# Differential attention: half-height tiles for the rotated parts, projections a head ahead, splits and values later

## The chip, the core and the metric

The kernel runs on one NeuronCore of a Trainium2 chip. The metric is the device time of one execution in microseconds. TensorE is called PE in the profile's rows (PEld is its weight load), VectorE DVE, ScalarE ACT, GpSimd POOL, and SP is the engine that issues the DMAs.

## The reference, cut to what matters

A trunk of two layers over 512 tokens of width 1024, in fp32. Each layer has a mixer, a cross-attention into 256 memory tokens, and a feed-forward part, each followed by a layer norm. The change touches the mixer of the second layer, differential attention with rotary positions, 8 heads of two 64-wide halves each, and the memory keys and values that are computed beside it.

```python
def odd_mixer(x, w_in, lam_p, subln_g, w_out, lam_init):
    q, k, v = jnp.split(x @ w_in, 3, axis=-1)
    q, k = rope(q), rope(k)              # 8 heads x 2 halves of 64
    o = diff_attention(q, k, v, lam)     # per head: softmax(q0 k0^T/8) - lam * softmax(q1 k1^T/8), times v (128 wide)
    o = rms_norm(o, subln_g) * (1.0 - lam_init)
    return o.reshape(B_, S, C_WIDTH) @ w_out

def memory_cross_attention(x, mem, wq, wkv, wo):
    k, v = jnp.split(mem @ wkv, 2, axis=-1)
    ...
```

## The kernel before

**Arithmetic.** To get more precision than one fp32r matmul gives, an operand is split into a high part (a cast to fp32r, on ScalarE) and a low part (the rest, a subtraction, on VectorE or GpSimd). A product of two split operands is three matmuls: high x high, high x low, low x high (`mm3`, lines 143 to 145). Weights arrive in chunks of 128 x 1024 (`chunk`, lines 131 to 139): one DMA into one of two `raw` buffers, a cast into one of five `whi` tiles, a subtraction into one of five `wlo` tiles. `tproj` (157) projects all 512 tokens to 128 features, `nproj` (182) tokens first.

**The odd layer** (`odd`, 838). The projections of heads 0 and 1 come first, then the memory tokens are loaded and split (`memory`, 692; into four `part` and four `kv` tiles), then the values of all heads (line 894). Each projected bank passes `rope` (850): a copy to `raw`, four DMAs that swap quarter rows, a multiplication by the cosines on VectorE, and two operations on GpSimd (lines 858 and 859) that give the rotated tile `m`. `project_q` and `project_k` split `m` at once: for each half c, `qh` holds the high part in both 64-row halves and `ql` the low part in both, while `kst` holds the key's high part in the rows of c and its low part in the other rows. That is six 128 x 512 tiles a head out of 13 `st` buffers. Two matmuls over 128 rows then give all four products (lines 949 and 950).

**The loop** (`diff_heads`, 931; `pipe`, 122). 8 heads x 4 query blocks are 32 units, in five stages: scores (row maximum on VectorE, exponential on ScalarE, combination), the normalisation `norm` (983), the product with the values `mix` (974), the transposes of the finished head `finish` (992), and the transposes of the probabilities `turn` (962). After each stage `fill` (107) takes work from a queue of jobs until an estimate of TensorE time has been used up: the stage's figure times `rate(i)`. Unit i means pass i of this loop. The queue holds, in this order: the memory keys of all four heads (`cross_k`), the projections of heads 2 to 6, the memory values (`cross_v`), the projections of head 7, and the first half of the output projection. `before` (906) makes sure at a head's third unit that the next head's projections are out.

The order in which the code issues operations is a priority: at build time they are put into the order of each engine's queue, and a tile that has no free buffer waits until one is released. On the chip each engine works through its queue.

The same trick with half-height operands appears in one other place, the neighbourhood attention of the first layer (line 1288), whose scores contract over 64 rows:

```python
            for u in range(2):
                rows = slice(u * 64, u * 64 + 64)
                nc.tensor.matmul(sb[u][:, :256], q[rows, g * P:(g + 1) * P], k[rows, k0 * 64:k0 * 64 + 256],
                                 start=True, stop=True)
```

Of the kernel before, what the change touches and what calls it, by code (L numbers as in the profile page):

```python
# [10 lines left out]
F32 = mybir.dt.float32  # L11
F32R = mybir.dt.float32r
AF = mybir.ActivationFunctionType
ALU = mybir.AluOpType
# [32 lines left out]
class Trunk:  # L47
# [3 lines left out]
    def __init__(self, ctx, tc, a, stop=6):  # L51
        self.tc, self.nc, self.a, self.stop = tc, tc.nc, a, stop
        self.n = 0
        e = ctx.enter_context
        self.dp = e(tc.tile_pool(name="dp", bufs=1, space=bass.MemoryType.DRAM))
        self.pp = e(tc.tile_pool(name="pp", bufs=1, space=PSUM))
        self.cp = e(tc.tile_pool(name="cp", bufs=1))
        self.wp = e(tc.tile_pool(name="wp", bufs=1))
        self.sp = e(tc.tile_pool(name="sp", bufs=1))
        self.gp = e(tc.tile_pool(name="gp", bufs=1))  # L60
        self.xtp = e(tc.tile_pool(name="xtp", bufs=1))
        self.lo_eng = tc.nc.vector
        self.jobs = []
        self.late = []
        self.xr = {}

# [32 lines left out]
    def step(self):  # L99
        j = self.jobs[0]  # L100
        cost = j.step()
        if j.done:
            self.jobs.pop(0)
            return 0.0
        return cost

    def fill(self, us):
        while us > 0 and self.jobs:
# [594 lines left out]
                    p.extend([x[:, :M], x[:, M:2 * M]])  # L703
        return parts

    def even_mem(self, mem):

        pairs = [[self.wp.tile([P, 1024], F32R, tag=t, bufs=5, name=self.nm("m" + t)) for t in ("whi", "wlo")]
                 for _ in range(2)]
        tiles = [x[:, u * 512:(u + 1) * 512] for p in pairs for u in range(2) for x in p]  # L710
        mem.extend(self.memory(lambda: tiles.pop(0)))
        yield 0.0
# [14 lines left out]
                self.nc.scalar.copy(kk[:, e * M:(e + 1) * M], b[:, :M])  # L727
            ks.append(kk)

    def cross_v(self, l, vs, mem):  # L730

        for h in range(2):
            bs = yield from self.nproj([self.a["wv"][l, h, i] for i in range(4)], 512, MB, *mem)
            for b in bs:
                v = self.kvblk()
                self.nc.scalar.copy(v, b)
                vs.append(v)
# [100 lines left out]
    def odd(self, l, mk, mv):  # L838
        nc, a = self.nc, self.a
        H = 8  # L840
        halves = (slice(0, 64), slice(64, 128))
        qs, ks, parts = [None] * (2 * H), [None] * (2 * H), []
        with self.phase("odd") as pool:
            tmp = self.tiles(pool)
            cos, sin = tmp("cos", 1), tmp("sin", 1)
            nc.sync.dma_start(cos, a["rope"][0])
            nc.sync.dma_start(sin, a["rope"][1])
            nlam, gc = self.lambdas(tmp("raw", 1))

            def rope(b):  # L850
                raw, sw, m = tmp("raw", 1), tmp("sw"), tmp("m")
                nc.scalar.copy(raw, b)
                for c in range(2):
                    lo, hi = slice(c * 64, c * 64 + 32), slice(c * 64 + 32, c * 64 + 64)
                    nc.sync.dma_start(sw[lo], raw[hi])
                    nc.sync.dma_start(sw[hi], raw[lo])
                nc.vector.tensor_tensor(m, b, cos, ALU.mult)
                nc.gpsimd.tensor_tensor(sw, sw, sin, ALU.mult)
                nc.gpsimd.tensor_tensor(m, m, sw, ALU.add)
                return m  # L860

            def project_q(h, b):
                m = rope(b)
                for c in range(2):
                    s, o = halves[c], halves[1 - c]
                    qh, ql = tmp("st", 13, dt=F32R), tmp("st", 13, dt=F32R)
                    for r in (s, o):
                        nc.scalar.activation(qh[r], m[s], AF.Copy, scale=0.125)
                    for r in (s, o):
                        nc.vector.scalar_tensor_tensor(ql[r], m[s], 0.125, qh[s].bitcast(F32), ALU.mult, ALU.subtract)  # L870
                    qs[2 * h + c] = (qh, ql)

            def project_k(h, b):
                m = rope(b)
                for c in range(2):
                    s, o = halves[c], halves[1 - c]
                    kst = tmp("st", 13, dt=F32R)
                    nc.scalar.copy(kst[s], m[s])
                    nc.vector.tensor_tensor(kst[o], m[s], kst[s].bitcast(F32), ALU.subtract)
                    ks[2 * h + c] = kst  # L880

            def projects(h):
                project_q(h, (yield from self.tproj(a["ow"][h])))
                project_k(h, (yield from self.tproj(a["ow"][H + h])))

            first = self.tproj_halves([a["ow"][0], a["ow"][H], a["ow"][1], a["ow"][H + 1]])
            for i, b in enumerate(first):
                (project_k if i % 2 else project_q)(i // 2, b)
            slots = [self.part] * 4 + [lambda: self.kvblk(F32R)] * 4
            mem = self.memory(lambda: slots.pop(0)())  # L890
            vs = []
            for h in range(2):
                row = []
                for b in self.run(self.nproj([a["ov"][h, i] for i in range(4)], 512, TB, tag=("at", "pj")[h])):
                    v = tmp("v", 8)
                    nc.scalar.copy(v, b)
                    row.append(v)
                vs.append(row)
            self.lo_eng = nc.vector
            self.job(self.cross_k(l, mk, mem))  # L900
            more = [self.job(projects(h)) for h in range(2, 7)]
            self.job(self.cross_v(l, mv, mem))
            more += [self.job(projects(h)) for h in range(7, H)]
            second = self.outproj(parts, KB, a["oout"], l, 0)

            def before(h):
                if 2 <= h < H:
                    self.need(more[h - 2])

            self.diff_heads(H, before, qs, ks, vs, nlam, gc, tmp, parts)  # L910
            self.lo_eng = nc.vector
        with self.phase("ln") as pool:
            second(pool)
# [14 lines left out]
        nc.vector.tensor_scalar(gc, gc, 1.0 - LAM_INIT, None, ALU.mult)  # L928
        return nlam, gc

    def diff_heads(self, H, before, qs, ks, vs, nlam, gc, tmp, parts):
        nc = self.nc

        def scores(n):
            h, t = n["h"], n["t"]
            if t == 2:
                before(h + 1)
            if t == 0:
                n["head"] = {"ssq": self.small(4, 4)}
            else:  # L940
                n["head"] = units[h * TB]["head"]
            tk = slice(t * P, (t + 1) * P)
            nm, sm = self.small(2), self.small(2)
            rc = n["rc"] = self.small(2, 8, "rc")
            ps = n["p"] = []
            for c in range(2):
                sb = self.bank()
                qh, ql = qs[2 * h + c]
                nc.tensor.matmul(sb, qh[:, tk], ks[2 * h + c], start=True, stop=False)
                nc.tensor.matmul(sb, ql[:, tk], ks[2 * h + c], start=False, stop=True)  # L950
                nc.vector.tensor_reduce(nm[:, c:c + 1], sb, AX.X, ALU.max, negate=True)
                p = tmp(f"p{c}", 3 - c)
                nc.scalar.activation(p, sb, AF.Exp, bias=nm[:, c:c + 1], accum_out=sm[:, c:c + 1])
                ps.append(p)
            nc.vector.reciprocal(rc, sm)
            nc.vector.scalar_tensor_tensor(rc[:, 1:2], rc[:, 1:2], nlam, sm[:, 0:1], ALU.mult, ALU.mult)
            nc.vector.scalar_tensor_tensor(ps[0], ps[1], rc[:, 1:2], ps[0], ALU.mult, ALU.add)
# [8 lines left out]
        def mix(n):  # L966
            h, t, hd = n["h"], n["t"], n["head"]
            tk = slice(t * P, (t + 1) * P)
            if t == 0:
                hd["on"] = tmp("on")  # L970
                hd["ob"] = self.bank()
            ob, ssq = hd["ob"], hd["ssq"]
            for j in range(TB):
# [12 lines left out]
        def finish(n):  # L986
# [4 lines left out]
            for j in range(TB):  # L991
# [5 lines left out]

        units = [{"h": h, "t": t} for h in range(H) for t in range(TB)]
        self.pipe(units, [(scores, 0, 1.0), (norm, 4, 0.0), (mix, 3, 1.4), (finish, 5, 0.0), (turn, 2, 1.3)],
                  lambda i: 1.1 if i < 22 else 0.9)  # L1000


    def even(self, l, mk, mv):
        nc, a = self.nc, self.a
        A = 4
        with self.phase("even") as pool:
# [72 lines left out]
            def project_b(hp):  # L1079
                for i in range(2):  # L1080
                    bqk[2 * hp + i] = tiled((yield from self.tproj(a["ebqk"][4 * i + hp])), tmp("qk", 18))

            mem = []
            bjobs = [self.job(g) for g in (project_v(), project_b(0), project_b(1), self.even_mem(mem), project_b(2))]
            kv = [self.job(g) for g in (self.even_k(l, mk, mem, 0), project_b(3), self.even_k(l, mk, mem, 1),
                                        self.even_v(l, mv, mem))]
            second = self.outproj(parts, KB, a["eout"], l, 0)
# [349 lines left out]
```

## Time and profile before

| | us |
|---|---|
| median of 3 runs | 1592.86 (1592.32 to 1599.11) |
| the profiled execution | 1595.57 |
| its span, first to last instruction | 1593.9 |
| mean granted TensorE clock, of full speed | 0.996 |

The profile is of one execution. Its span lies 1.7 us under that execution's own time; the median of the other runs lies 2.7 us under it. A matmul's record lasts longer than the time it takes from its neighbours, since matmuls are pipelined: the pitch from start to start is what a matmul costs.

### The profile page before, as it was taken

To read this page: it belongs to the slowest core of one execution; us is meant where nothing else is said; L and a number is where in the kernel's file an instruction comes from. 1 tells how busy PE (TensorE), PEld (TensorE's weight loads), DVE (VectorE), ACT (ScalarE), POOL (GpSimd) and SP (SyncE) were. 2 spreads that over 40 slices of the span, in tenths; PEclk is the share of its full clock that TensorE was granted. 3 is DMA by queue.
4 is the path that set the end of the run, shared out by engine and by line. 5 is a ranking of instruction groups with operands and counts; after the bars stand their busy time and mean duration, and the time that the engine had idled before them with its cause. 6 is when DMAs were issued, how large, how long until landed. Compare 5 with 4: busy or idle time off the path is not lost.

```text
span 1593.9 us, 24998 instructions
## 1 busy us (share of the span) xinstructions
PE 1561.3 (98%) x9668; PEld 1375.4 (86%) x9668; DVE 1163.3 (73%) x1892; ACT 785.4 (49%) x1465; POOL 262.1 (16%) x263
## 2 busy tenths in 40 slices
PE   8999999999999999999999999989999999999997
PEld 7877887898899999988898977767988999999886
DVE  4684445475499989898766588776745998988986
ACT  4684455244255555445245566663442655554450
POOL 0012000221220000014131144232212100000151
PEclk9999999999999999999999999999999999999999
DMA  5432343442333333353254433403413333333531
GB/s 166 141 98 75 101 145 126 171 135 76 134 120 119 106 101 103 103 211 93 80 181 132 131 88 93 132 27 119 146 53 146 119 120 103 104 103 102 198 93 66
DMA packets 59415, 185.89 MB, mean 117 GB/s; under 512 B 7680, under 2 KB 7840, under 8 KB 59296
## 3 DMA queue, kind: packets, MB, share of 16 engines
q1 hardware_dynamic: 59296, 184.30, 35.7%
q8 instruction: 76, 1.25, 0.3%
q14 instruction: 43, 0.35, 0.1%
HBM read 167.47 MB, written 12.60 MB: 113 GB/s over the span
## 4 chain that ended last, share of the span: by engine, by line
PE 35%; DVE 6%; ACT 3%; POOL 2%; DMA 2%; issue 2%; SPq 0%; POOLq 0%; DVEq 0%; ACTq 0%
PE pj L143 3%; PE pj L145 3%; PE pj L144 3%; PE at L661 3%; PE pj L416 2%; PE pj L417 2%; PE at L531 2%; PE pj L418 2%; PE pj L531 2%; PE at L416 2%; PE at L417 2%; PE at L418 2%; PE at L143 2%; PE at L144 2%; PE at L145 2%
## 5 line engine op out<-in xcount | busy, mean ns | idle before, releaser
L137 ACT CAST whi<-raw 128x1024 fp32r<-128x1024 f32 (+2 forms) x158 | 159.3, 1009 | 194.8 <-PE pj L144 67.2
L138 DVE TENSOR_TENSOR wlo<-raw,whi 128x1024 fp32r<-128x1024 f32 (+2 forms) x142 | 170.3, 1202 | 110.6 <-ACT whi L137 104.1
L143 PE MATMUL pj<-xh,whi 128*128 128x512 f32 (+1 forms) x640 | 228.0, 356 | 0.0
L145 PE MATMUL pj<-xh,wlo 128*128 128x512 f32 (+1 forms) x640 | 216.9, 339 | 0.6 <-DVE wlo L138 0.6
L144 PE MATMUL pj<-xl,whi 128*128 128x512 f32 (+1 forms) x640 | 216.5, 338 | 0.0
L397 ACT CAST whi<-sump 128x512 fp32r<-128x512 f32 x160 | 97.6, 621 | 113.3 <-issue 64.4
L143 PEld LDWEIGHTS pj<-xh,whi 128*128 128x128 f32 x640 | 120.7, 189 | 15.7 <-issue 5.2
L144 PEld LDWEIGHTS pj<-xl,whi 128*128 128x128 f32 x640 | 120.7, 189 | 14.7 <-issue 3.8
L145 PEld LDWEIGHTS pj<-xh,wlo 128*128 128x128 f32 x640 | 120.4, 188 | 14.8 <-DVE wlo L138 0.8
L401 DVE TENSOR_TENSOR wlo<-sump,whi 128x512 fp32r<-128x512 f32 x160 | 107.7, 688 | 13.3 <-ACT whi L397 13.1
L397 ACT CAST whi<-raw 128x512 fp32r<-128x512 f32 x120 | 72.2, 617 | 32.2 <-PE at L417 14.8
L581 POOL TENSOR_TENSOR s<-kv 128x256 f32<-128x256 f32 x12 | 14.6, 1235 | 439.5 <-DVE o L435 434.8
L401 DVE TENSOR_TENSOR wlo<-raw,whi 128x512 fp32r<-128x512 f32 x120 | 81.2, 688 | 0.5
L220 POOL TENSOR_SCALAR s<-s 128x1 f32<-128x1 f32 x56 | 26.0, 464 | 310.8 <-DVE s L306 167.9
L416 PE MATMUL at<-xh,whi 128*128 128x256 f32 x240 | 67.8, 283 | 2.6 <-DVE o L431 2.6
L416 PE MATMUL pj<-xh,whi 128*128 128x256 f32 x240 | 68.3, 285 | 1.3 <-DVE o L431 1.3
L417 PE MATMUL pj<-xl,whi 128*128 128x256 f32 x240 | 67.9, 283 | 0.0
L417 PE MATMUL at<-xl,whi 128*128 128x256 f32 x240 | 67.9, 283 | 0.0
L418 PE MATMUL at<-xh,wlo 128*128 128x256 f32 x240 | 67.8, 283 | 0.0
L138 POOL TENSOR_TENSOR wlo<-raw,whi 128x1024 fp32r<-128x1024 f32 x16 | 38.3, 2392 | 179.6 <-ACT whi L137 179.6
L418 PE MATMUL pj<-xh,wlo 128*128 128x256 f32 x240 | 67.8, 282 | 0.0
L143 PE MATMUL pj<-whi,part 128*128 128x512 f32 x144 | 59.5, 413 | 0.0
(396 smaller groups left out, 4849.5 us busy)
## 6 DMA issues: line engine op xcount, KB each, us to landing
raw<-gu SPq DMA_DIRECT2D x88, 512.0 KB
raw<-down SPq DMA_DIRECT2D x22, 512.0 KB
xd<-x SPq DMA_DIRECT2D x40, 256.0 KB
x<-xd SPq DMA_DIRECT2D x20, 512.0 KB
raw<-wk SPq DMA_DIRECT2D x16, 512.0 KB
raw<-wv SPq DMA_DIRECT2D x16, 512.0 KB
raw<-wq SPq DMA_DIRECT2D x16, 512.0 KB
raw<-wo SPq DMA_DIRECT2D x16, 512.0 KB
```

The costliest lines, as they stand in the source:

```text
L137: nc.scalar.copy(hi[:, :w], raw[:, :w])
L138: (eng or self.lo_eng).tensor_tensor(lo[:, :w], raw[:, :w], hi[:, :w].bitcast(F32), ALU.subtract)
L143: mm(out, lh, rh, start=first, stop=False)
L144: mm(out, lh, rl, start=False, stop=False)
L145: mm(out, ll, rh, start=False, stop=last)
L397: nc.scalar.copy(n[p, "w"][0], n[p])
L401: nc.vector.tensor_tensor(lo, n[p], hi.bitcast(F32), ALU.subtract)
L416: mm(out, hi[:, c], th[k], start=first, stop=False, skip_group_check=True)
L417: mm(out, hi[:, c], tl[k], start=False, stop=False, skip_group_check=True)
L418: mm(out, lo[:, c], th[k], start=False, stop=k == 3, skip_group_check=True)
L531: mm(bank, s[:, tk], w[:, c], start=first and j == n == 0, stop=j == 1 and n == 2, skip_group_check=True)
L661: mm(out[p][t], l_[:, tk], r[:, wk], start=c == k == n == 0 and p in ("p1", "p5"), stop=k == 1 and n == 2, skip_group_check=True)
```

## The change

- **Tiles.** `q` of a half c becomes one tile: high part in the rows of c, low part in the other rows. The key becomes `kh` (high part in both row halves, one tile for each c) and `kl` (low parts of both c, in their own rows, one tile for both). Five tiles a head, 14 `st` buffers. The first score matmul contracts over 128 rows (q high x k high and q low x k high), the second over the 64 rows of c (q high x k low). The product low x low falls away.
- **Later splits.** `later` puts the four split steps of a projection on a list, due 9.0 us of emitted filler after it and 1.2 us apart; `step` advances that clock by each job's estimate and issues what is due; `flush` issues what a head still lacks where its scores begin.
- **Order of the jobs.** The projections of heads 2 to 5 alternate with one memory key each, then come the projections of heads 6 and 7, then the memory values. The rate is 1.05 throughout.
- **Memory tokens.** They are split into two pairs of weight tiles (`early_mem`, the renamed `even_mem`), after the values' projections.
- **`on`**, the normalised head, has one buffer in place of two.

```diff
+    def later(self, owner, delay, apart, *work):
+
+        at = max([self.clock + delay] + [s[0] + apart for s in self.soon])
+        self.soon += [(at + i * apart, owner, f) for i, f in enumerate(work)]
+
+    def flush(self, owner):
+        while any(s[1] == owner for s in self.soon):
+            self.soon.pop(0)[2]()
...
             def project_q(h, b):
                 m = rope(b)
-                for c in range(2):
-                    s, o = halves[c], halves[1 - c]
-                    qh, ql = tmp("st", 13, dt=F32R), tmp("st", 13, dt=F32R)
-                    for r in (s, o):
-                        nc.scalar.activation(qh[r], m[s], AF.Copy, scale=0.125)
-                    for r in (s, o):
-                        nc.vector.scalar_tensor_tensor(ql[r], m[s], 0.125, qh[s].bitcast(F32), ALU.mult, ALU.subtract)
-                    qs[2 * h + c] = (qh, ql)
+
+                def high(c):
+                    s = halves[c]
+                    qs[2 * h + c] = tmp("st", 14, dt=F32R)
+                    nc.scalar.activation(qs[2 * h + c][s], m[s], AF.Copy, scale=0.125)
+
+                def low(c):
+                    s, o, q = halves[c], halves[1 - c], qs[2 * h + c]
+                    nc.vector.scalar_tensor_tensor(q[o], m[s], 0.125, q[s].bitcast(F32), ALU.mult, ALU.subtract)
+
+                self.later(h, 9.0, 1.2, *[f for c in range(2) for f in (lambda c=c: high(c), lambda c=c: low(c))])
...
+                def high(c):
+                    s = halves[c]
+                    kh = tmp("st", 14, dt=F32R)
+                    ks[2 * h + c] = kh, (tmp("st", 14, dt=F32R) if c == 0 else ks[2 * h][1])
+                    for r in (s, halves[1 - c]):
+                        nc.scalar.copy(kh[r], m[s])
+
+                def low(c):
+                    s, (kh, kl) = halves[c], ks[2 * h + c]
+                    nc.vector.tensor_tensor(kl[s], m[s], kh[s].bitcast(F32), ALU.subtract)
...
-            self.job(self.cross_k(l, mk, mem))
-            more = [self.job(projects(h)) for h in range(2, 7)]
+            self.run(self.early_mem(mem))
+            more = []
+            for h in range(2, H):
+                more.append(self.job(projects(h)))
+                if h < 6:
+                    self.job(self.cross_k(l, mk, mem, [h - 2]))
             self.job(self.cross_v(l, mv, mem))
-            more += [self.job(projects(h)) for h in range(7, H)]
...
+                self.flush(h)
...
-                qh, ql = qs[2 * h + c]
-                nc.tensor.matmul(sb, qh[:, tk], ks[2 * h + c], start=True, stop=False)
-                nc.tensor.matmul(sb, ql[:, tk], ks[2 * h + c], start=False, stop=True)
+                q, (kh, kl), s = qs[2 * h + c], ks[2 * h + c], halves[c]
+                nc.tensor.matmul(sb, q[:, tk], kh, start=True, stop=False)
+                nc.tensor.matmul(sb, q[s, tk], kl[s], start=False, stop=True)
...
-                hd["on"] = tmp("on")
+                hd["on"] = tmp("on", 1)
...
-                  lambda i: 1.1 if i < 22 else 0.9)
+                  lambda i: 1.05)
```

## Rows read from the trace of the kernel before

**Rows 1.** The page's engine table: busy us, share of the span, instructions.

```profile
PE 1561.3 (98%) x9668; PEld 1375.4 (86%) x9668; DVE 1163.3 (73%) x1892; ACT 785.4 (49%) x1465; POOL 262.1 (16%) x263
```

**Rows 2.** Windows: busy us and instructions of each engine, granted clock, DMA.

```profile
core 0: us, PE busy (x) PEld busy (x) DVE busy (x) ACT busy (x) POOL busy (x), PEclk, DMA share, GB/s
866.00:1097.00 231.00, 216.64 (x1210) 181.78 (x1209) 168.39 (x275) 145.69 (x325) 73.96 (x92) 0.99 0.33 102
...
1047.00:1060.00 13.00, 7.92 (x39) 6.98 (x38) 10.61 (x21) 8.30 (x23) 3.97 (x6) 0.75 0.13 40
1060.00:1097.00 37.00, 33.10 (x199) 26.26 (x198) 22.38 (x50) 22.69 (x63) 10.91 (x23) 1.00 0.26 100
```

**Rows 3.** Waits of TensorE, 840 to 1110 us: total us, times, longest.

```profile
PE at L962 <- ACT p L953: 5.6, 2, 5.1
PE at L949 <- ACT p L953: 3.1, 2, 1.7
PE at L974 <- DVE on L983: 2.4, 4, 0.7
PE pj L992 <- ACT kv L736: 1.8, 1, 1.8
```

**Rows 4.** Timeline near 950 us, ScalarE and TensorE: start, us, operation, idle before.

```profile
950.69 1.27 ACT L868 ACTIVATE st<-m 64x512 fp32r<-64x512 f32 x2 [2.36 <-POOL m L859]
...
952.82 0.50 PE L949 MATMUL at<-st,st 128*128 128x512 f32 x1 [1.69 <-ACT p L953]
```

**Rows 5.** Timeline from 1049 to 1055 us, VectorE, ScalarE and TensorE.

```profile
1049.45 1.39 DVE L870 SCALAR_TENSOR_TENSOR st<-m,st 64x512 fp32r<-64x512 f32 x2
...
1053.70 0.69 ACT L953 ACTIVATE p<-at,s 128x512 f32<-128x512 f32 x1 [2.38 <-DVE s L951]
...
1054.53 1.12 PE L962 MATMUL at<-ident,p 128*128 128x128 f32 x4 [5.08 <-ACT p L953]
```

**Rows 6.** Timeline of TensorE, first and last of 17 instructions after that stall.

```profile
1055.30 0.78 PE L949 MATMUL at<-st,st 128*128 128x512 f32 x1
...
1059.71 0.87 PE L962 MATMUL at<-ident,p 128*128 128x128 f32 x4
```

**Rows 7.** Timeline of TensorE, the first of four score matmuls and their successor.

```profile
942.46 0.39 PE L949 MATMUL at<-st,st 128*128 128x512 f32 x1
...
943.37 0.40 PE L143 MATMUL pj<-xh,whi 128*128 128x512 f32 x1
```

**Rows 8.** Timeline of TensorE around the half-height matmuls of line 1288.

```profile
215.02 0.40 PE L145 MATMUL pj<-xh,wlo 128*128 128x512 f32 x1
215.35 0.70 PE L1288 MATMUL at<-qk,qk 64*128 64x256 f32 x4
215.98 0.50 PE L143 MATMUL pj<-xh,whi 128*128 128x512 f32 x1
216.32 0.40 PE L144 MATMUL pj<-xl,whi 128*128 128x512 f32 x1
```

**Rows 9.** Narrow windows inside another such group: its two pairs, the next load.

```profile
226.68 0.49 PE L1288 MATMUL at<-qk,qk 64*128 64x256 f32 x2
...
227.00 0.38 PE L1288 MATMUL at<-qk,qk 64*128 64x256 f32 x2
...
227.31 0.19 PEld L143 LDWEIGHTS pj<-mwhi,whi 128*128 128x128 f32 x1 [0.33 <-issue]
```

**Rows 10.** Timeline of TensorE, full-height fp32 transposes after an fp32r matmul.

```profile
930.99 0.39 PE L145 MATMUL pj<-xh,wlo 128*128 128x512 f32 x1
931.22 0.60 PE L992 MATMUL pj<-ident,on 128*128 128x128 f32 x4
```

**Rows 11.** Groups of ScalarE and VectorE, 866 to 1097 us: busy, mean ns, idle before.

```profile
L868 ACT ACTIVATE st<-m 64x512 fp32r<-64x512 f32 x24 | 15.1, 631 | 10.2 <-POOL m L859 9.8
...
L870 DVE SCALAR_TENSOR_TENSOR st<-m,st 64x512 fp32r<-64x512 f32 x24 | 18.2, 758 | 4.7 <-PE at L949 3.1 <-ACT st L868 1.4
```

**Rows 12.** Window of the first layer with memory tokens in the weight tiles.

```profile
205.00:275.00 70.00, 70.00 (x431) 55.84 (x429) 38.23 (x62) 37.94 (x89) 0.00 (x0) 1.00 0.38 122
```

**Rows 13.** Timeline of TensorE in the drain of the loop.

```profile
1087.15 1.13 PE L974 MATMUL at<-v,at 128*128 128x128 f32 x8 [0.71 <-DVE on L983]
```

## What the change will do to the time

> **What bounds the kernel now.** I read the page's engine table first: TensorE is busy for 1561 of 1594 us [rows 1], so at most some 33 us of the whole kernel are waits of TensorE, and every other gain or loss has to come from the time that TensorE needs for its own instructions. Then I cut out the stretch that the change touches, the loop over heads from 866 to 1097 us [rows 2]: 231 us, TensorE busy for 216.6 of them, VectorE for 168, ScalarE for 146, GpSimd for 74. TensorE is the bound there, with 14.4 us of idle time, 5.1 of it in the 13 us from 1047 to 1060 and 3.9 in the last 37 us. The view of waits names what ended that idle time [rows 3]: exponentials of ScalarE (5.6 and 3.1 us), the normalisation of VectorE (2.4 us), and one copy of a values bank (1.8 us). The timeline says why the exponentials were late, in two places:
>
> Around 950 us GpSimd is still at the rotated sum `m` of line 859; ScalarE has the first split copy of it (line 868) in hand and stands for 2.36 us, the exponential is queued behind it, and TensorE, which needs the score bank that this exponential empties, stands for 1.69 us [rows 4]. The other 1.4 us of the 3.1 in [rows 3] come in the same way ten microseconds later, with VectorE's splits in front of a reduction. Around 1050 us the splits of the last head come late: VectorE does two multiply-subtracts and two subtracts (lines 870, 879) while a reduction of scores is queued behind them, the exponential comes 2.38 us late and TensorE stands for 5.08 us [rows 5]. After that stall the granted clock is 0.75 on average over the 13 us [rows 2], and the 4.4 us from 1055.30 to 1059.71, in which the matmul records are long [rows 6], hold work that at 2.4 GHz would take about half, so 2.2 us more are lost to the 1.2 GHz level. Sum of these stalls: 1.7 + 1.4 + 5.1 + 2.2 = 10.4 us. The rest of the idle time (6.2 us) has other causes: normalisation in the drain of the loop, the values bank, small change.
>
> **The change, part by part.**
>
> *Later splits, a head ahead.* A head is four units of 3.7 x 1.05 = 3.9 us of emitted filler work, 15.5 us; one head's two projections (2 x 8 x 0.65 = 10.4) and one memory key (16 x 0.325 = 5.2) add up to 15.6, so one head's projections are issued in each head's time, some 1.3 heads before use. The splits follow 9 us of filler later, well past the rotation chain, and at the latest where the head's scores begin. With that the waits of [rows 4] and [rows 5] lose their cause; for the last head the splits fall at about unit 22 to 25 and are wanted at unit 28, where they now come at the last moment. I take the whole 10.4 us off. The lower bound of this gain is nothing, if ScalarE and VectorE are late for another reason at the same places; what is late next would be the exponential behind a reduction. In all, ScalarE's split copies waited 10.2 us in one of their two groups [rows 11], which is more than what reached TensorE.
>
> *Five tiles.* ScalarE keeps six half-height copies a head (two for q, four for k in place of four and two). VectorE loses two multiply-subtracts a head: of the 24 in this stretch 12 go, 12 x 0.758 = 9.1 us [rows 11]. VectorE is not the bound (73% busy), so I book nothing beyond the stalls above. The 14 buffers hold two heads of five and four tiles of a third, so a split no longer waits for the scores of an earlier head.
>
> *The second score matmul becomes half-height.* This is the term that decides. Before, lines 949 and 950 contract over 128 rows; four of them and a neighbour follow each other every 0.23 us (0.91 us for four) [rows 7]. After, line 949 still does, while the second takes rows 0 to 63 for c = 0 and 64 to 127 for c = 1, with a full-height matmul before and after it: 32 units x 2 = 64 times full, half, full. The trace of before has half-height matmuls in one place, line 1288, among full-height 512-column ones [rows 8]. The last full one starts at 215.02 and the next would be due at 215.25; the half-height group starts at 215.35, 0.10 late. It holds TensorE until 215.98, 0.63 us, and the first full one after it needs 0.34 us until its successor instead of 0.23, 0.11 too many. Inside such a group [rows 9] there are two pairs, each on both halves at once: the second pair starts 0.32 us after the first, and the following full-height weight load starts only with its matmul at 227.31, 0.31 us after the second pair: nothing is loaded ahead across the border. A group of one instruction therefore holds TensorE for 0.31 us (one pitch, lower end) to 0.63 - 0.21 = 0.42 us (the whole group less the streaming of one pair). With the 0.10 and the 0.11 this is 0.52 to 0.63 us in place of 0.23: 0.29 to 0.40 more, and 64 x that is 18.6 to 25.6 us. Line 1288 is plain fp32, the new matmul is fp32r; but the full-height fp32 transposes of line 992 follow an fp32r matmul after 0.23 us, with no delay [rows 10], so it is the height and not the type. I take the middle, 0.35 us, 22.4 us in all. A gain below nothing is excluded, because the two halves that could run side by side are never neighbours.
>
> The Trainium skill has this as a rule that speaks against the change: "TensorEngine Tiling (Array Packing)", section "Key Properties", says that a change of tiling mode, unlike a change of tile, drains the TensorE. The trace agrees with it by the 0.10 us and the load that is not pulled ahead, named above; by that page each of the 64 matmuls would pay two drains, on which it puts no figure.
>
> *Memory tokens in the weight buffers.* `early_mem` takes two of the five pairs of weight tiles until the values are done, and runs after the first values' projections instead of before; its loads pass the eight `ov` loads in SP's queue and its four subtractions move on GpSimd to a time when that has room (74 of 231 us busy). Three pairs are left for the chunks. The even layer does just this, and from 205 to 275 us TensorE is busy 70.00 of 70 us [rows 12], so I book nothing; if that cover failed (VectorE is busier here), each late chunk would cost about 1 us, the time of a split.
>
> *Values last* moves 20.8 us of filler from units 18 to 23 to units 22 to 27; the total to be filled is the same, the last quarter of the output projection still has to wait for head 7, so the drain after 1060 keeps its 3.9 us idle. The wait for a values bank (1.8 us) may stay too. Booked at nothing.
>
> *One buffer for the normalised head.* Line 983 of a head's first tile now waits for the transposes of the head before (line 992), which are emitted after it; line 974 of the next tile waits for line 983 because it writes the same bank. Nearest row: line 974 waiting 0.71 us on line 983 where nothing fills in [rows 13]. There are seven such borders; 0 to 5 us, and since filler stands between I take 2 us.
>
> Sum: 22.4 - 10.4 + 2.0 = +14.0 us. The profiled execution took 1595.57 us with a span of 1593.9; its neighbours' median is 1592.86. So span about 1608, that execution about 1609.6, and the median of runs **1607 us**.
>
> **Rivals.**
>
> *A, the border is free and the change is faster.* If a half-height fp32r matmul costs the same 0.23 us, only the stalls count: -10.4 + 2 = -8.4 us, 1584.5. Its place are the 64 matmuls, its point of decision 8.4 / 64 = 0.13 us each: below that the change gains. For it: the profile has no half-height fp32r matmul. Against: [rows 8] to [rows 10]. The Trainium skill has this too: "TensorE: Matmul & The Clock Gate", section "Why this matters for your kernels", says that a single matmul of few rows takes the time of a full one. That fits the streaming in [rows 9] and says nothing of the border; no run shows it for fp32r. Chance 0.14.
>
> *B, the cost fits into what is idle.* The lower end of the cost and all 14.4 + 2.2 us of idle time and slow clock but the drain's 3.9 gone: 18.6 - 12.7 = +5.9, 1599. For it: longer units give ScalarE and VectorE more time. Against: TensorE is idle only 6% of the stretch, most of it in single places. Chance 0.16.
>
> *C, the stalls stay.* The splits wait elsewhere or the flush at a head's start stands in front of its scores: 22.4 + 2 = +24.4, 1617; with the upper price +27.6, 1620. For it: ScalarE and VectorE work in order and are 60 to 70% busy. Against: 9 us of filler is longer than the rotation chain. Chance 0.16.
>
> **How the numbers follow.** The forecast (1601 to 1613) has 0.54. The range from 1587 to 1616 leaves out about half of A and the upper half of C. A measurement of this kernel can tell about 0.5%, 8 us, from no change: faster (under 1585) is half of A and little else, 0.10; within 0.5% is the other half of A and most of B, 0.19; slower is the rest, 0.71.
>
> **What would show it.** Right: in the timeline of the new kernel the second score matmul starts about 0.3 us after the first, its weight load starts with it, and the next full one starts 0.3 to 0.4 us later; the stretch grows to about 245 us with TensorE's idle time below 10 us; no split copy of ScalarE waits for line 859; no 5 us stall and no 1.2 GHz level near the last head. Wrong: a pitch of 0.23 us around the half-height matmul (then A), waits of TensorE on line 983 of a microsecond or more at each head (the single buffer costs more than I took), or weight chunks that come late.

## The result and the profile after

| | before | after |
|---|---|---|
| median of the runs, us | 1593.96 (1592.32 to 1599.11, 4 runs) | 1605.8 (1605.3 to 1607.7, 4 runs) |
| span of the profiled execution, us | 1593.9 | 1603.5 |
| mean granted TensorE clock | 0.996 | 0.999 |

The changed kernel takes 1.0075 times as long, with a 95% interval of 1.0063 to 1.0087: 11.8 us more, where 14 were forecast. TensorE's time of work grew, and its waits became fewer. The page's engine table of the kernel after, against [rows 1]:

```profile
PE 1579.8 (99%) x9668; PEld 1369.8 (85%) x9668; DVE 1146.1 (71%) x1876; ACT 785.6 (49%) x1465; POOL 261.4 (16%) x263
```

The loop over heads now ends 10 us later. Its windows, with the columns of [rows 2]:

```profile
866.00:1107.00 241.00, 235.65 (x1208) 177.65 (x1207) 160.03 (x265) 148.31 (x326) 72.58 (x92) 1.00 0.33 101
...
1047.00:1060.00 13.00, 13.00 (x65) 10.19 (x64) 7.87 (x13) 9.70 (x21) 3.87 (x4) 1.00 0.33 112
```

TensorE is idle for 241 - 235.65 = 5.4 us of it, against 14.4 before; the stall near the last head and the 1.2 GHz level behind it are gone. VectorE has 16 instructions less, as the edit says (1892 to 1876). The waits of TensorE, 840 to 1115 us, against [rows 3] (line 1001 was 974, 1010 was 983, 1019 was 992, 989 was 962, 980 was 953):

```profile
PE at L1001 <- DVE on L1010: 4.2, 6, 1.5
PE at L1019 <- DVE on L1010: 0.6, 1, 0.6
PE at L989 <- ACT p L980: 0.5, 3, 0.2
```

The exponentials hold TensorE for 0.5 us in place of 8.7. What costs the time is in the timeline of TensorE at a unit's scores (line 976 is the full-height matmul, 977 the half-height one), which answers [rows 7]:

```profile
947.36 0.40 PE L976 MATMUL at<-st,st 128*128 128x512 f32 x1
947.69 0.49 PE L977 MATMUL at<-st,st 64*128 64x512 f32 x1
948.11 0.50 PE L976 MATMUL at<-st,st 128*128 128x512 f32 x1
948.54 0.50 PE L977 MATMUL at<-st,st 64*128 64x512 f32 x1
948.97 0.39 PE L157 MATMUL pj<-mwhi,whi 128*128 128x256 f32 x1
```

From start to start 0.33, 0.42, 0.43 and 0.43 us, 1.61 us for the four, where [rows 7] had 0.91. The next matmul pays too, as the same place in another unit shows, with a 512-column neighbour:

```profile
940.51 0.50 PE L977 MATMUL at<-st,st 64*128 64x512 f32 x1
940.93 0.50 PE L157 MATMUL pj<-xh,whi 128*128 128x512 f32 x1
941.27 0.39 PE L158 MATMUL pj<-xl,whi 128*128 128x512 f32 x1
```

0.34 us until its successor, 0.11 over 0.23. Together (1.61 - 0.91 + 0.11) / 2 = 0.40 us for each half-height matmul. The weight loads of the same place show what is different: each of the first three starts with its own matmul, at 940.07, 940.50 and 940.93, and the load engine stands idle before it:

```profile
940.07 0.19 PEld L976 LDWEIGHTS at<-st,st 128*128 128x128 f32 x1 [0.25 <-issue]
940.50 0.18 PEld L977 LDWEIGHTS at<-st,st 64*128 64x128 f32 x1 [0.24 <-issue]
940.93 0.19 PEld L157 LDWEIGHTS pj<-xh,whi 128*128 128x128 f32 x1 [0.25 <-issue]
941.04 0.19 PEld L158 LDWEIGHTS pj<-xl,whi 128*128 128x128 f32 x1
```

Only the load at 941.04, full height after full height, starts ahead of its matmul (941.27). A pitch of 0.42 to 0.43 us is 0.19 to 0.20 over 0.23, about the length of one load's record (0.18 to 0.19), which fits a load that nothing covers. That is the picture of [rows 9], now for fp32r. It fits what the Trainium skill calls a drain at a change of tiling mode ("TensorEngine Tiling (Array Packing)", "Key Properties"); the figure, which the page leaves open, is 0.40 us here for a change there and back.

### The profile page after: what moved, and what is told of

Its sections match the earlier page's. It is cut to its first block, busy times and chain, and to the rows that moved or that the text cites. A ratio compares the mean times of both kernels' runs of the same rounds, so it can differ in the third digit from the quotient of the medians.

```text
span 1603.5 us, 24970 instructions
## 1 busy us (share of the span) xinstructions
PE 1579.8 (99%) x9668; PEld 1369.8 (85%) x9668; DVE 1146.1 (71%) x1876; ACT 785.6 (49%) x1465; POOL 261.4 (16%) x263
## 4 chain that ended last, share of the span: by engine, by line
PE 41%; DVE 5%; ACT 1%; POOL 1%; issue 1%; DMA 1%; SPq 0%; POOLq 0%; DVEq 0%; ACTq 0%
PE pj L157 4%; PE pj L159 4%; PE pj L158 4%; PE at L675 3%; PE pj L430 2%; PE pj L431 2%; PE pj L432 2%; PE at L430 2%; PE at L431 2%; PE at L432 2%; PE at L545 2%; PE pj L545 2%; PE at L1001 2%; PE at L157 2%; PE at L158 2%; PE at L159 2%
## 5 line engine op out<-in xcount | busy, mean ns | idle before, releaser
L980 ACT ACTIVATE p<-at,s 128x512 f32<-128x512 f32 x64 | 43.7, 685 | 37.0 <-DVE s L978 34.5
```

## The experiments

All differences below are ratios to the kernel before, times 1594 us. The first four runs, the next four and the last three were each taken on one chip, with the kernel before beside them. A difference between groups, or to the changed kernel, is a difference of two such ratios; it is said where their intervals overlap.

### The second score matmul at full height again

The shared tile `kl` holds the low parts of both halves, so its other 64 rows only add a term of the size of low x low.

```diff
-                nc.tensor.matmul(sb, q[s, tk], kl[s], start=False, stop=True)
+                nc.tensor.matmul(sb, q[:, tk], kl, start=False, stop=True)
```

> The changed kernel with the second score matmul at full height again: q[:, tk] x kl in place of q[s, tk] x kl[s]. The one shared kl tile holds the low key parts of both halves c, so the extra rows add q low of c times k low of the other c, a term as small as the low x low products that are left out. Theory 1 (the half-height matmul between full-height ones costs 0.36 to 0.41 us more): 64 x that, 23 to 26 us, go away: 1580 to 1583 us, some 0.7% under the kernel before, and a pitch of 0.23 us at the second score matmul. Rival 2 (the loss comes from the new order, the weight buffers or the single buffer of the normalised head): 1603 to 1606 us.

Measured: 1595.0 us, ratio 1.0008 (0.9999 to 1.0017), that is 10.7 us under the changed kernel and not the 23 to 26 of theory 1, though far outside rival 2. The timeline has the 0.23 us pitch back, so TensorE did get its time back; but of the 64 x 0.40 = 25.6 us more than half did not reach the end. The waits of TensorE, 840 to 1110 us, are 13.7 us in place of 5.3:

```profile
PE at L1001 <- DVE on L1010: 11.9, 8, 4.4
PE at L989 <- ACT p L980: 1.2, 2, 0.7
PE at L1019 <- DVE on L1010: 0.6, 1, 0.6
```

Line 1010 writes the normalised head `on`, which has one buffer. The longest of these waits, in the timeline of all engines:

```profile
916.51 2.54 ACT L898 CAST st<-m 64x512 fp32r<-64x512 f32 x4 [3.43 <-POOL m L873]
...
917.22 0.60 PE L1019 MATMUL pj<-ident,on 128*128 128x128 f32 x4
...
919.08 0.69 ACT L980 ACTIVATE p<-at,s 128x512 f32<-128x512 f32 x1
...
920.56 0.17 DVE L982 RECIPROCAL rc<-s 128x2 f32<-128x2 f32 x1 [0.79 <-ACT p L980]
...
921.77 1.23 DVE L152 TENSOR_TENSOR wlo<-raw,whi 128x1024 fp32r<-128x1024 f32 x1
...
922.91 0.41 DVE L1010 TENSOR_SCALAR on<-at,s,rc 128x128 f32<-128x128 f32 x1
...
923.37 1.86 PE L1001 MATMUL at<-v,at 128*128 128x128 f32 x7 [4.42 <-DVE on L1010]
```

The transposes that free the buffer are over at 917.8, yet line 1010 runs at 922.91. Its place in VectorE's queue, settled at build time, is behind a reciprocal that waits for an exponential, which itself stands behind the split copies that wait for the rotation. The single buffer put line 1010 far back in an ordered queue, and TensorE's next values product behind it. The clock falls after it: 0.94 on average from 920 to 950 us.

### The half-height matmuls as neighbours

```diff
+            sbs = [self.bank(), self.bank()]
             for c in range(2):
...
+                nc.tensor.matmul(sbs[c], qs[2 * h + c][:, tk], ks[2 * h + c][0], start=True, stop=False)
+            for c in range(2):
+                s = halves[c]
+                nc.tensor.matmul(sbs[c], qs[2 * h + c][s, tk], ks[2 * h + c][1][s], start=False, stop=True)
```

> The changed kernel with the four score matmuls in another order: both full-height ones, then the half-height ones of rows 0 to 63 and of rows 64 to 127 as neighbours. Theory 1a (what costs is the border between full and half height): one group instead of two a unit, and the two halves side by side; from the rows of line 1288 a group of one pair takes 0.10 + 0.42 + 0.11 = 0.63 us in place of 2 x 0.23 = 0.46, so 32 x 0.17 = 5.4 us more than full height: about 1587 us. Theory 1b (a half-height matmul is slow by itself, about 0.43 us, whoever its neighbour is): one after the other 1604 to 1606 us.

Measured: 1595.13 us, ratio 1.0009 (1.0000 to 1.0018), the same as full height, with the same waits on the normalised head (8.0 us), and far from the numbers of both theories. That speaks for the border and against a slow half-height matmul, but with those waits in it the size can't be read; it was repeated without them below.

### The kernel before with half height alone

```diff
-                nc.tensor.matmul(sb, ql[:, tk], ks[2 * h + c], start=False, stop=True)
+                s = slice(c * 64, c * 64 + 64)
+                nc.tensor.matmul(sb, ql[s, tk], ks[2 * h + c][s], start=False, stop=True)
```

> The kernel before with this one edit: its second score matmul at half height, ql[s, tk] x kst[s], which leaves out low x low. Theory 1: 64 x 0.36 to 0.41 = 23 to 26 us more, of which up to 6 us may fall into TensorE's idle time: 1612 to 1620 us, with the 5 us stall near the last head still there. Rival 2 (the height costs nothing): 1594 us.

Measured: 1609.75 us, ratio 1.0102 (1.0088 to 1.0116): 16.3 us more, 2 under the expected range. One edit makes the kernel before slower than the whole change does, with the same pitch of 0.43 us in its timeline (line 951 is the half-height matmul). From 64 x 0.40 = 25.6 us some 9 did not reach the end; 7 of them show as idle time of TensorE that is gone, 7.3 us in the loop in place of 14.4. The waits at 950, 960 and 1008 us of [rows 3] are gone, the stall near the last head is not.

```profile
948.60 0.50 PE L951 MATMUL at<-st,st 64*128 64x512 f32 x1
949.03 0.50 PE L949 MATMUL at<-st,st 128*128 128x512 f32 x1
```

```profile
PE at L963 <- ACT p L954: 4.6, 2, 4.4
PE at L975 <- DVE on L984: 2.1, 3, 0.7
```

### Two buffers for the normalised head

```diff
-                hd["on"] = tmp("on", 1)
+                hd["on"] = tmp("on")
```

and 13 `st` buffers in place of 14, for the space.

> The changed kernel with two buffers for the normalised head again, paid for with 13 st buffers in place of 14 (two heads of five tiles still fit). If the single buffer is what makes line 1001 wait for line 1010 inside the loop (1.5, 0.8 and 0.4 us at 926, 963 and 1032 us), these three waits go and the time falls by 2 to 3 us, to about 1603; if they come from the wait of the normalisation for GpSimd, nothing changes (1605 to 1607).

Measured: 1602.18 us, ratio 1.0059 (1.0044 to 1.0075): 2.5 us under the changed kernel, with intervals that overlap. The waits on line 1010 inside the loop (1.5, 0.8 and 0.4 us) are gone; the two that are left are in its drain. The edit also takes one `st` buffer away, and no run separates the two.

```profile
PE at L1001 <- DVE on L1010: 1.2, 2, 0.6
```

### Full height and two buffers

> The changed kernel with both edits: the second score matmul at full height, and two buffers for the normalised head (13 st buffers). Theory 1 (the border costs some 0.38 us each, the single buffer made the waits that stood in its place in e1_full: 9.7 us of line 1001 on line 1010 inside the loop, and the 1.2 GHz level after them): 1602.2 less 24 us, with up to 5 us of other waits coming up, 1578 to 1584. Rival 3 (other waits take their place whatever the buffer, because VectorE and ScalarE set the pace once TensorE is shorter): 1590 to 1595, as e1_full.

Measured: 1585.54 us, ratio 0.9939 (0.9926 to 0.9951), 9.7 us under the kernel before: both edits together beat both kernels. Against the runs with one of them, the second buffer (with one `st` buffer less) is worth 0.0069 x 1594 = 11.0 us where the matmul is full height, and the height is worth 0.0120 x 1594 = 19.1 us where there are two buffers. Of the waits on line 1010 only those in the drain are left, and the longest wait of TensorE is for the low part of a weight chunk:

```profile
PE pj L158 <- DVE wlo L152: 2.3, 1, 2.3
PE at L1001 <- DVE on L1010: 1.9, 3, 0.7
```

The first two of four score matmuls and the next one behind them, in its timeline, 0.92 us for the four:

```profile
946.31 0.39 PE L976 MATMUL at<-st,st 128*128 128x512 f32 x1
946.54 0.39 PE L977 MATMUL at<-st,st 128*128 128x512 f32 x1
...
947.23 0.40 PE L157 MATMUL pj<-xh,whi 128*128 128x512 f32 x1
```

### The border itself, with two buffers

> As e8_full_on2, but with the half-height matmuls as neighbours (order of e2_pair). Theory 1a (the border costs): 32 groups a 0.17 to 0.25 us more than full height, 5 to 8 us over e8_full_on2, far from the 18 to 24 us that separate it from half-height ones between full ones. Theory 1b (a half-height matmul is slow by itself): as e6_on2, 1602.

Measured: 1588.55 us, ratio 0.9962 (0.9949 to 0.9974): 3.7 us over full height by the ratios, with intervals that touch, and 15.5 under half height between full ones. The timeline:

```profile
947.85 0.62 PE L975 MATMUL at<-st,st 128*128 128x512 f32 x2
948.40 0.50 PE L978 MATMUL at<-st,st 64*128 64x512 f32 x2
948.83 0.50 PE L157 MATMUL pj<-xh,whi 128*128 128x512 f32 x1
949.16 0.39 PE L158 MATMUL pj<-xl,whi 128*128 128x512 f32 x1
```

Both half-height matmuls, recorded in 0.50 us together, hold TensorE from 948.40 to 948.83, 0.43 us, as long as a single one did above. With 0.09 us ahead and 0.10 behind that is 0.62 us for a pair, against 0.46 for two full-height ones: 0.16 a unit, 32 x 0.16 = 5 us. So a half-height matmul is not slow; going in and out is.

### Splits at once

```diff
-        at = max([self.clock + delay] + [s[0] + apart for s in self.soon])
-        self.soon += [(at + i * apart, owner, f) for i, f in enumerate(work)]
+        for f in work:
+            f()
```

> As e8_full_on2, but the splits are issued right behind the rotation, as in the kernel before. If the 9 us of delay keep the exponentials free, the stalls of 1 to 2 us at the projections come back: 3 to 8 us over e8_full_on2. If the order of the jobs and the five tiles alone do it: the same within 2 us.

Measured: 1586.52 us, ratio 0.9955 (0.9940 to 0.9971). The interval overlaps that of the delayed splits: the delay is worth 2.6 us by the ratios, and anything between nothing and some 5 us fits. It does not keep ScalarE free. Waits of ScalarE in full height with two buffers, where the splits are delayed:

```profile
ACT st L882 <- POOL m L873: 13.1, 5, 4.4
ACT st L898 <- POOL m L873: 11.4, 5, 3.8
```

24.5 us of waiting for the rotation, and 23.5 without the delay, against 17.4 in the kernel before: 9.8 in [rows 11] and the first line below. In the changed kernel itself, where TensorE is slower, they are the other two lines, 14.4 us: a little less than before, and far from none.

```profile
ACT st L878 <- POOL m L859: 7.6, 3, 3.2
...
ACT st L898 <- POOL m L873: 8.2, 3, 3.8
ACT st L882 <- POOL m L873: 6.2, 3, 3.6
```

### The order of the jobs as before

Full height, two buffers, delayed splits, but the queue and the rate of the kernel before.

> As e8_full_on2, but with the order of the jobs and the rate of the kernel before: all memory keys first, the projections of heads 2 to 6, the memory values, then head 7. If the late projection of head 7 made the 5.1 us stall with its 2.2 us at 1.2 GHz, the time is 4 to 8 us over e8_full_on2 and the stall stands near the last head; if the delayed splits or the five tiles removed it, the same within 2 us.

Measured: 1589.98 us, ratio 0.9973 (0.9962 to 0.9983): 5.4 us over the new order. There is no single 5 us stall; the loss is in small waits along the loop (exponentials 2.4 us in 5 waits and 1.6 in 2, a copy of transposes 2.3 in 3). So it was not the lateness of the last projection alone that made the stall.

### The order alone, the tiles alone

The kernel before with the new job order, rate and place of the memory tokens, and six tiles a head:

> The kernel before with the new order of the jobs, the rate of 1.05 and the memory tokens in the weight buffers; six tiles a head, splits at once, two buffers for the normalised head as before. If the order alone makes the gain that the full-height runs show (e8_full_on2 is 0.6% under the kernel before), 1585 to 1588 us. If it needs the smaller tiles as well, because a third head's splits wait for st buffers or VectorE has 16 operations more, 1589 to 1594.

Measured: 1591.68 us, ratio 0.9982 (0.9973 to 0.9992), 2.9 us less. Then five tiles alone, full height, everything else as before:

> The kernel before with five tiles a head alone (full-height matmuls, 13 st buffers, two buffers for the normalised head, splits at once, jobs and memory tokens as before). e11_full_on2_order differs from this only in the delayed splits and the memory tokens and took 0.27% less than the kernel before: if the tiles do that, 1588 to 1591 us; if not, 1593 to 1595, with the 5 us stall near the last head.

Measured: 1588.96 us, ratio 0.9967 (0.9954 to 0.9980), 5.3 us less. The stall near the last head falls apart into waits of at most 0.9 us, though the splits here are not delayed and the jobs have the old order:

```profile
1049.30 0.66 PE L989 MATMUL at<-ident,p 128*128 128x128 f32 x4 [0.93 <-ACT p L980]
```

The run of the section before this one has the five tiles and the old order too, with the delayed splits and the tokens in the weight buffers; its ratio is 0.9973, so these two add nothing there that can be told. One place where six tiles cost time shows in the run with the order alone, whose longest wait of TensorE (4.14 us at 949.75) ends this chain:

```profile
941.85 1.39 POOL L858 TENSOR_TENSOR sw<-sw,sin 128x512 f32<-128x512 f32 x1 [2.58 <-DMA sw<-raw]
...
942.00 4.89 DVE L870 SCALAR_TENSOR_TENSOR st<-m,st 64x512 fp32r<-64x512 f32 x4
...
943.31 1.62 POOL L859 TENSOR_TENSOR m<-m,sw 128x512 f32<-128x512 f32 x1
...
946.90 1.39 DVE L879 TENSOR_TENSOR st<-m,st 64x512 fp32r<-64x512 f32 x2
...
948.21 1.28 DVE L952 TENSOR_REDUCE s<-at 128x1 f32<-128x512 f32 x2
...
949.75 0.50 PE L950 MATMUL at<-st,st 128*128 128x512 f32 x1 [4.14 <-ACT p L954]
```

A head's query splits occupy VectorE for 4.9 us in one piece, and the reduction that the exponential needs is behind them. The first two of the four take 3.5 us together, while GpSimd is at the rotation, the last two 1.4. The kernel before has such a piece too, ahead of the wait of 1.44 us that ends at 962.19:

```profile
954.77 4.53 DVE L870 SCALAR_TENSOR_TENSOR st<-m,st 64x512 fp32r<-64x512 f32 x4
959.34 1.39 DVE L879 TENSOR_TENSOR st<-m,st 64x512 fp32r<-64x512 f32 x2
960.64 1.28 DVE L951 TENSOR_REDUCE s<-at 128x1 f32<-128x512 f32 x2
```

Five tiles halve the number of these multiply-subtracts. They also need fewer buffers; but VectorE waits for a free `st` tile for 2.7 us in the loop with five tiles and for 3.1 before ([rows 11]), so little of the gain shows there. No run separates the two.

### Memory tokens as before

> As e8_full_on2, but with the memory tokens in the part and kv tiles and loaded before the values' projections, as in the kernel before, so that all five pairs of weight buffers serve the chunks. If three pairs are too few, the 2.3 us wait of a projection for a low weight part at 1011 us goes and the time falls by 2 to 4 us below e8_full_on2; if VectorE's queue is what made that chunk late, the same within 2 us.

Measured: 1588.92 us, ratio 0.9966 (0.9952 to 0.9980): slower than with the tokens in the weight buffers, by 4.3 us at the middle, with intervals that just part. The wait for the weight part went, and another came at 1022 us, for a projection bank that VectorE's last step of a finished head had not left:

```profile
PE pj L157 <- DVE part L1023: 4.1, 1, 4.1
```

The trace is of the longest of the five executions, 1594.44 us, so whether the others have this wait is not known. Three pairs of weight buffers may have caused the wait for the weight part, but five pairs do not make the kernel faster. Which of the two differences, place or time of the loads, makes it slower stays open.

## Why the prediction came out as it did

**The bound** was named rightly: TensorE is busy for 98% of the stretch after, and the time moved with its own work.

**The half-height matmul** is the term that decided, by the mechanism that was forecast. Its price for TensorE was 0.29 to 0.40 us by the bounds, 0.35 taken; 0.40 was measured, the upper end: the weight load of a single half-height matmul is as uncovered as that of a group. (The upper bound took 0.21 us off a group for the streaming of a pair, a figure that none of its rows shows; the pitch of 0.42 to 0.43 us bears the bound out.) The row of line 1288 in another layer, another type and another width carried over. In time it came to 19 us where TensorE had little else to wait for, 16 in the kernel before, 11 in the change with its single buffer: the rest fell into waits. The sum added it to the waits as if they were independent.

**The single buffer**: 2 us booked out of 0 to 5, 2.5 measured, which the intervals do not tell from nothing and the 2.7 us of waits that went bear out. But that is its price behind a slow TensorE. Next to full-height matmuls it is 11 us, outside the bounds. The bound came from a row of the drain, a wait of 0.71 us at each border; in the loop the write of the normalised head can stand behind a whole chain in VectorE's queue, as the wait of 4.42 us shows. One cost hid the other; each removed alone gives 2.5 or 10.7 us, both together 21.7.

**The stalls**: 10.4 us booked as a gain, and the change without its two costs is 9.7 us faster than the kernel before. The size held, the step that was to give it did not. The sign "no split copy of ScalarE waits for line 859" (873 now) did not come: the splits that were put off by 9 us of filler wait 14.4 us for the rotation in the changed kernel, against 17.4 before, and 24.5 once its two costs are away. The delay itself is worth between nothing and some 5 us. What gave more is what was booked at nothing, "VectorE is not the bound (73% busy), so I book nothing beyond the stalls": five tiles alone give 5.3 us and take the stall near the last head away, since a busy share of 73% says nothing of a piece of 4.5 us in front of a reduction. The order of the jobs gives 2.9 us alone (with the rate and the place of the memory tokens) and 5.4 on top of the tiles and the delay. So it is in part luck that 9.7 came out so near 10.4.

**The memory tokens** were booked at nothing. No harm of their new place shows; the run with the old one was slower.

**The sum** by ratios: -9.7 for the rest of the change, +19.1 for half height, +2.5 for the single buffer behind it, +11.9 in all, with the booked -10.4, +22.4 and +2.0 beside it. (The three are steps of one chain of runs, so they must add up; what they test is the single terms.) Rival A fails on the pitch, B on the price, C because the stalls did go.

## What to carry to other kernels

Count how often TensorE changes between matmuls over 128 rows and over 64: the saved rows bring nothing, and each change there and back cost 0.40 us; padding with a small term took all of it away, and making two half-height matmuls on opposite rows neighbours left 0.16 us for a pair. A buffer taken from a tile that an ordered queue writes may cost little while another engine is slow and several times as much once it is not, so undo costs in pairs before one is called small. And where an engine is 70% busy, look for its longest uninterrupted piece in front of the critical instruction before you book its savings at nothing.

## What was not expected of the hardware

Two half-height matmuls of 512 columns on opposite rows held TensorE for 0.43 us together, no longer than one alone between full-height neighbours (0.42 to 0.43 us). And four multiply-subtracts of 64 x 512 on VectorE took 4.89 us in one place: 3.5 us for the two that ran while GpSimd was at the rotation, 1.4 for the two behind it, where the same line's mean over the loop of the kernel before was 0.76 ([rows 11]). That GpSimd is the reason is likely from this place alone, and no run tests it.
